# Stick-breaking scores: keys held once as high and low part, queries as two operands of 128 rows

## The chip, the cores and the metric

The kernel runs on one core of a Trainium2 chip. The metric is the time of one execution on the device in microseconds (us). Five engines work from queues of their own: TensorE (PE; its weight loads are listed as PEld), VectorE (DVE), ScalarE (ACT), GpSimd (POOL) and SyncE (SP), which issues most of the DMAs.

## The reference

One hybrid decoder block on x of (1, 1024, 1024): an RMS norm, one input projection, eight heads of strictly causal stick-breaking attention beside eight heads of latent attention (MLA), an output projection, a gated MLP with a short convolution, and a gated embedding. The part that the change touches is the score z of the stick-breaking heads:

```python
def stick_breaking_attention(q, k, v):
    scale = SB_HEAD_DIM ** -0.5                       # SB_HEAD_DIM = 64
    for start in range(0, seq, Q_BLOCK):              # 8 blocks of 128 queries
        end = start + Q_BLOCK
        z = jnp.einsum('bqhd,bkhd->bhqk', q[:, start:end], k[:, :end]) * scale
        strict = s_idx < t_idx
        log_keep = jnp.where(strict, -jax.nn.softplus(z), 0.0)
        log_keep_after = lax.cumsum(log_keep, axis=3, reverse=True) - log_keep
        weights = jnp.where(strict, jnp.exp(jax.nn.log_sigmoid(z) + log_keep_after), 0.0)
        outs.append(jnp.einsum('bhqk,bkhd->bqhd', weights, v[:, :end]))
```

## The kernel before

Every float32 operand of a product is held as the sum of two float32r parts, high and low (`split`, L90: ACT casts the high part at L93, DVE subtracts it from the source at L94). A product of two such operands is high by high, low by high and high by low. `mm3` (L115) does it in three matmuls.

Stage 1 (L203) normalises and transposes x into `hTh` and `hTl`, makes the latents, and the keys and values of the first pair of heads. Stage 2 begins with the stick-breaking heads: four pairs c of heads, each with two heads e, each with two halves g of the queries, which makes 16 units in the order c, e, g. `sb_softmax` (L624) makes the weights of a unit, one block of 128 queries after the other: the scores go to a PSUM bank (L636, L637 and, for the piece with the diagonal, the mask of L447), ACT takes two sigmoids of them (L640, L641), DVE scans the first along the keys (L643) and multiplies (L645). `weighted_sum` (L451) transposes the weights (L459), splits them (`th`, `tl`) and multiplies them with the values (L473, L474); DVE writes the unit's output `o` (L479), and after the last unit of a pair POOL sends it to the DRAM (L674). `run_units` writes the scores of a unit between the steps of the weighted sum of the unit before it.

Into the steps of both, `fill` mixes other work by rates: `project` (L224), which makes 128 columns of the input projection in 24 matmuls for each half `th` of the tokens, for the queries, keys and values of the next pair (`to_q`, `to_k`, `to_v`; `sb_pre`, L651, adds the three), and `mla_prepare` (L546). The last order on each engine is set by a scheduler from priorities; a fill has its priority put off by `LATER`.

The head dimension is 64, so a pair's projection holds head 0 in partitions 0 to 63 and head 1 in 64 to 127 (`hs`). For head e before the change, the key tile `ka` or `kb` has the high part of the keys in both halves of its 128 partitions (the second is a copy, L259), the low parts of both heads lie in a third tile `kl`, which takes its slot from the tag `ka` or `kb` by turns, and the query tile `qa` or `qb` has the high part in the head's own half and the low part in the other. The first product (L636) takes all 128 rows, which is high by high and low by high; the second (L637) takes the 64 rows of the head, high by low:

```python
pe.matmul(sc, q[:, qs], k[:, c0:c1], start=True, stop=False)               # L636
pe.matmul(sc, q[rows, qs], kl[rows, c0:c1], start=False, stop=c1 < n)      # L637
```

The MLA heads follow (stage 2, second part), with scores of 96 rows in three products (L1064 to L1066) and the same mask line L447; then the MLP and the embedding. The change doesn't touch these.

Of the kernel before, what the change touches and what calls it, by code (L numbers as in the profile page):

```python
# [18 lines left out]
P = 128  # L19
S = 1024  # L20
D = 1024
NT = 8          # token tiles
NK = 8          # chunks of D_MODEL
H = 512         # tokens of a half
HD = 64
DFF = 2816
NCH = DFF // P  # 22
# [8 lines left out]
# how the work between the steps of the attention is spread: steps of it per step  # L36
# [5 lines left out]
# how far the scheduler is to put it behind the attention  # L42
LATER = (500, 0, 0, 2000)
# tiles normalised together in each half, and those scaled on the scalar engine
# [5 lines left out]
def tile_hybrid_block(ctx: ExitStack, tc: tile.TileContext, a: dict, out: bass.AP):  # L50
# [39 lines left out]
    def split(h, l, src, gain=None, on_pool=False):  # L90
        """src (times a gain of each partition) as the sum of two float32r parts."""
        if gain is None:
            act.copy(h, src)  # L93
            (pool if on_pool else dve).tensor_tensor(l, src, h, ALU.subtract)  # L94
        else:
            act.activation(h, src, AF.Copy, scale=gain)
            dve.scalar_tensor_tensor(l, src, gain, h, ALU.mult, ALU.subtract)
# [9 lines left out]
    def split_w(src, width=512, gain=None, on_pool=False, where=None):  # L107
        """A weight block of the DRAM, split."""
        w = load_w(src, width)
        wh = (where or stage).tile([P, 512], F32R, tag="wh", name=nm("wh"), bufs=4)  # L110
        wl = (where or stage).tile([P, 512], F32R, tag="wl", name=nm("wl"), bufs=4)
        split(wh[:, :width], wl[:, :width], w[:, :width], gain, on_pool)
        return wh, wl
# [6 lines left out]
    def rstd_dve(small, ssq, count, n, tag, bufs=None):  # L120
        """(ssq / count + eps) ** -0.5 on one engine: Newton steps from a guess by exponent."""
# [16 lines left out]
    def rotate(eng, p_, x1, x2, cs, sn, shape):  # L138
        """The rotation of the pairs (x1, x2), in place."""
# [11 lines left out]
    class Fill:  # L151
        """Work traced in small steps between those of a stage. A generator gives True where it
        leaves none of the stage's buffers open."""
# [6 lines left out]
        def add(self, g, later=0):  # L160
            """later: how far behind the rest the scheduler is to put this work."""
            self.gens.append((g, later))
# [32 lines left out]
    now = {}                    # the current stage's makers of banks and of small tiles  # L195
# [17 lines left out]
    def sb_tiles(c):  # L213
        """Keys of two heads twice, their low parts, values; queries come later."""
        t4 = lambda tag: ata.tile([P, S], F32R, tag=tag, name=nm(tag), bufs=3)
        ka, kb = t4("ka"), t4("kb")
        kl = t4("ka" if c % 2 == 0 else "kb")
        vt = [ata.tile([P, NT, P], F32R, tag="v", name=nm("v"), bufs=3) for _ in range(2)]
        return {"k": (ka, kb), "kl": kl, "v": vt}
# [4 lines left out]
    def project(ci, consume, ths=(0, 1), ws=None):  # L224
        """128 columns of the input projection, transposed, for each half of the tokens."""
# [16 lines left out]
    def to_q(tiles):  # L242
        """Queries: the high part beside the low part."""
        def consume(th, ps):
            if th == 0:
                tiles["q"] = (tile4("qa", 2), tile4("qb", 2))
            sl = slice(th * H, th * H + H)
            for e in range(2):
                q = tiles["q"][e]
                split(q[hs[e], sl], q[hs[1 - e], sl], ps[hs[e], :])  # L250
        return consume

    def to_k(tiles):
        def consume(th, ps):
            sl = slice(th * H, th * H + H)
            for e in range(2):
                k = tiles["k"][e]
                split(k[hs[e], sl], tiles["kl"][hs[e], sl], ps[hs[e], :])
                act.copy(k[hs[1 - e], sl], k[hs[e], sl])  # L259
# [17 lines left out]
    with tc.tile_pool(name="pre", bufs=1) as pre, \  # L277
# [29 lines left out]
        # masks (rows are queries, columns keys)  # L307
# [7 lines left out]
        def normed(th):  # L315
            """A half of the tokens normalised, transposed and split."""
# [28 lines left out]
        # rotary tables  # L345
# [38 lines left out]
        def latents(th):  # L384
            """The latents of a half of the tokens, normalised, their keys' part rotated."""
# [14 lines left out]
            # the narrower part's sum doubled, so that one mean serves both  # L400
# [48 lines left out]
    def weighted_sum(u, p_, ptr, pav, rate):  # L449
        """The transposed product of a unit's weights with its values."""  # L450
# [30 lines left out]
        # the columns divided by their sums of weights: a row of each, the same in every partition  # L481
# [8 lines left out]
    def run_units(units, softmax, p_, ptr, pav, rates):  # L490
        """Softmax of each unit traced between the steps of the sum before it."""
# [52 lines left out]
    def mla_prepare(kv_only):  # L544
        """Latents to keys, values (kv_only) or queries of all MLA heads, kept in the DRAM."""
# [66 lines left out]

    for z in (project(0, to_q(pairs[0])), mla_prepare(False)):
# [10 lines left out]
    def sb_softmax(u):  # L624
        rows = hs[u["e"]]
        g, w = u["g"], u["w"]
        z = u["tiles"]
        q, k, kl = z["q"][u["e"]], z["k"][u["e"]], z["kl"]
        for i in range(4 * g, 4 * g + 4):
            n = (i + 1) * P  # L630
            qs = slice(i * P, i * P + P)
            kc = kcs[flip[0] % 2]
            flip[0] += 1
            for c0, c1 in pieces(n):
                sc = one_bank(py, "sc")[:, :c1 - c0]
                pe.matmul(sc, q[:, qs], k[:, c0:c1], start=True, stop=False)  # L636
                pe.matmul(sc, q[rows, qs], kl[rows, c0:c1], start=False, stop=c1 < n)  # L637
# [13 lines left out]
    def sb_pre(u):  # L651
        c, g, e = u["c"], u["g"], u["e"]
        if e == 0 and g == 0:
            fill.drain()
            sb_pre.o = atb.tile([P, S], F32, tag="o", name=nm("o"), bufs=2)
            if c < 3:
                z = sb_tiles(c + 1)
                pairs.append(z)
                for ci, f_ in ((c + 1, to_q), (c + 5, to_k), (c + 9, to_v)):
# [25 lines left out]
    # --- MLA heads; between them the output projection of the stick-breaking heads, then of the  # L685
    # --- MLA heads' first half of the tokens, then the FFN of this half
# [11 lines left out]
    def group_ssq(src, sq, s, ps):  # L698
        """Sums of the squares over the features of (128, 4, 128) in token layout."""
# [6 lines left out]
    def o_tile(c0, t):  # L706
        """Four chunks of features of a token tile."""
# [4 lines left out]
    def group_rstd(c0, ts):  # L712
        """Reciprocal roots of the mean squares of a group of features, one column a tile."""
# [13 lines left out]
    def group_product(c0, ts, consume):  # L727
        """A group of features times its rows of w_o."""
# [22 lines left out]
    def out_proj_sb(th, rows):  # L751
        """The stick-breaking heads' part of the output projection for a half of the tokens."""
# [8 lines left out]
    def out_proj_mla(th, rows, h2):  # L761
        """The rest of the output projection for a half of the tokens, residual and norm."""
# [40 lines left out]
    def embed(th, z):  # L803
        """Per-layer embeddings of a half of the tokens, kept in the DRAM."""
# [34 lines left out]
    def by_turns(a_, b_, rate):  # L839
        """Two generators, rate steps of the second for one of the first."""  # L840
# [9 lines left out]
    def f_tile(c):  # L850
        """A slot for a chunk of the FFN's hidden features (in pairs where a slot holds two)."""
# [13 lines left out]
    def ffn_up(th, h2, f):  # L865
# [10 lines left out]
        for c in range(NCH):  # L876
# [46 lines left out]
            if now.get("light"):  # L923
                # the same function with the tables that are loaded
# [12 lines left out]
    with tc.tile_pool(name="mla", bufs=1, side="right", reuse_waits="tile") as ml:  # L937
# [3 lines left out]
        # what the first unit needs lies where the stick-breaking heads are done early  # L941
# [4 lines left out]
        def mt(tag, shape, dt, bufs):  # L946
            """A tile of one of the bufs slots tag0, tag1 ... by turns; the first with the
            early ones."""
# [193 lines left out]
    def norm_transposed(row, t, dst):  # L1142
        """A normalised token tile, transposed and split."""
# [11 lines left out]
    def residual(row, xt, gain, dst):  # L1155
        """x + norm(row) * gain, kept in row and stored."""
# [67 lines left out]
    # the gate's weights stay on chip: some blocks in the stage, the rest where the FFN was  # L1224
# [117 lines left out]
```

## Time and profile before

| | us |
|---|---|
| median of 3 runs (1587.54 to 1591.46) | 1590.11 |
| span of the profiled execution, first to last instruction; the page gives no other time of it | 1588.5 |
| PE busy in the span | 1507.7 (95%) |
| DVE busy in the span | 1079.6 (68%) |
| ACT busy in the span | 844.2 (53%) |
| stick-breaking units, first score product to last output | 104.4 to 418.3 |

Times in rows are counted from the start of the span. PE's matmuls are pipelined and their ends are modelled, so how long a matmul holds PE is better read from the start of one to the start of the next than from its own time. DVE and ACT work through their instructions one by one, so their busy times are work.

### The profile page before, as it was taken

What the parts mean: (1) busy time and instruction counts of PE and PEld (TensorE: products, weight loads), DVE (VectorE), ACT (ScalarE), POOL (GpSimd) and SP (SyncE); (2) the same over time, 40 slices, a digit from 0 to 9 for tenths busy, and PEclk for the clock granted to TensorE, in tenths of its full rate; (3) what the DMA queues carried; (4) which work ended last, traced back from release to release, by engine and by line L of the source; (5) the groups of instructions that cost most, each with busy time, mean ns of one, the idle gap of its engine ahead of it and who ended that gap; (6) DMA issues with size and microseconds to landing.
All of it is one profiled execution on the core that took longest, in us unless ns stands there. A gap on an engine that the chain in (4) does not pass through costs nothing. (4 is left out here: it accounts for less than half of the span.)

```text
span 1588.5 us, 20809 instructions
## 1 busy us (share of the span) xinstructions
PE 1507.7 (95%) x7032; PEld 1214.6 (76%) x7032; DVE 1079.6 (68%) x2021; ACT 844.2 (53%) x1649; POOL 271.1 (17%) x313
## 2 busy tenths in 40 slices
PE   4998999999899897999999999999999999999996
PEld 3976877766678786778888888888888888888875
DVE  4558667799767868866567954544986556544698
ACT  6345555677667756645544544444554444444542
POOL 7104300002133425242113100000000000000033
PEclk9998999999889999999999999999999999999998
DMA  6031210113345525134445532333443323333455
GB/s 197 22 100 40 86 48 27 41 52 126 111 134 148 157 70 186 61 99 146 148 125 169 177 119 90 97 95 96 141 134 94 98 94 94 93 93 94 132 176 169
DMA packets 109211, 173.78 MB, mean 109 GB/s; under 512 B 10912, under 2 KB 47680, under 8 KB 109104
## 3 DMA queue, kind: packets, MB, share of 16 engines
q1 hardware_dynamic: 100400, 142.71, 29.7%
q0 software_dynamic: 8704, 29.74, 5.0%
q8 instruction: 55, 0.90, 0.2%
q14 instruction: 52, 0.43, 0.1%
HBM read 142.26 MB, written 30.15 MB: 109 GB/s over the span
## 5 line engine op out<-in xcount | busy, mean ns | idle before, releaser
L93 ACT CAST wh<-ws 128x512 fp32r<-128x512 f32 x296 | 183.1, 620 | 213.3 <-PE mm L891 105.8
L94 DVE TENSOR_TENSOR wl<-ws,wh 128x512 fp32r<-128x512 f32 x281 | 199.9, 713 | 139.7 <-ACT wh L93 74.5
L889 PE MATMUL mm<-bh,wh 128*128 128x512 f32 x456 | 180.2, 395 | 0.0
L891 PE MATMUL mm<-bh,wh 128*128 128x512 f32 x456 | 180.1, 395 | 0.0
L94 DVE TENSOR_TENSOR fl<-f,fh 128x512 fp32r<-128x512 f32 x88 | 60.7, 691 | 118.0 <-PE mm L118 77.4
L94 DVE TENSOR_TENSOR tl<-tr,th 128x512 fp32r<-128x512 f32 x192 | 103.2, 549 | 33.9 <-ACT th L93 32.8
L895 PE MATMUL mm<-bh,wl 128*128 128x512 f32 x456 | 126.0, 396 | 0.0
L93 ACT CAST th<-tr 128x512 fp32r<-128x512 f32 x192 | 90.7, 483 | 64.6 <-PE tr L459 49.4
L643 DVE TENSOR_TENSOR_SCAN kc<-kc,one_f 128x128 f32<-128x128 f32 (+3 forms) x64 | 89.2, 1394 | 36.4 <-ACT kc L640 35.7
L93 ACT CAST fh<-f 128x512 fp32r<-128x512 f32 x88 | 54.6, 622 | 110.0 <-PE mm L117 84.3
L1160 POOL DMA_DIRECT2D x_dram<-fd x8 | 4.3, 538 | 615.1 <-DVE fd L1159 582.2
L459 PE MATMUL tr<-ident,w 128*128 128x128 f32 x576 | 103.3, 290 | 4.4 <-DVE tl L94 2.0
L889 PEld LDWEIGHTS mm<-bh,wh 128*128 128x128 f32 x456 | 85.9, 188 | 19.9
L891 PEld LDWEIGHTS mm<-bh,wh 128*128 128x128 f32 x456 | 85.9, 188 | 19.9
L895 PEld LDWEIGHTS mm<-bh,wl 128*128 128x128 f32 x456 | 85.6, 188 | 19.7
L116 PE MATMUL mm<-wh,fh 128*128 128x512 f32 x242 | 95.6, 396 | 0.0
L117 PE MATMUL mm<-wl,fh 128*128 128x512 f32 x242 | 95.3, 394 | 0.0
L459 PEld LDWEIGHTS tr<-ident,w 128*128 128x128 f32 x576 | 74.8, 148 | 20.0 <-DVE tl L94 3.7
L474 PE MATMUL av<-tl,v 128*128 128x512 f32 x192 | 75.8, 398 | 13.8 <-DVE tl L94 13.1
L473 PE MATMUL av<-th,v 128*128 128x512 f32 x192 | 79.2, 412 | 6.6 <-ACT th L93 3.6
L118 PE MATMUL mm<-wh,fl 128*128 128x512 f32 x242 | 82.5, 395 | 0.0
L640 ACT ACTIVATE kc<-sc 128x384 f32<-128x384 f32 (+4 forms) x96 | 47.7, 496 | 38.3 <-PE sc L447 22.9
(427 smaller groups left out, 3833.2 us busy)
## 6 DMA issues: line engine op xcount, KB each, us to landing
ws<-in_w_up SPq DMA_DIRECT2D x176, 256.0 KB, 2.6
ws<-in_w_down SPq DMA_DIRECT2D x88, 256.0 KB, 2.6
ws<-in_w_o SPq DMA_DIRECT2D x32, 256.0 KB, 2.8
xl<-x_dram SPq DMA_DIRECT2D x16, 512.0 KB, 3.9
ws<-in_w_in SPq DMA_DIRECT2D x24, 256.0 KB, 2.7
t<-o_dram SPq DMA_DIRECT2D x24, 256.0 KB, 3.2
xl<-o_dram SPq DMA_DIRECT2D x24, 256.0 KB, 2.8
xt<-in_x SPq DMA_DIRECT2D x8, 512.0 KB, 5.3
```

The lines of the kernel that those rows point to most:

```text
L93: act.copy(h, src)
L94: (pool if on_pool else dve).tensor_tensor(l, src, h, ALU.subtract)
L116: pe.matmul(ps, lh, rh, start=start, stop=False)
L117: pe.matmul(ps, lh, rl, start=False, stop=False)
L118: pe.matmul(ps, ll, rh, start=False, stop=stop)
L459: pe.transpose(tr[:, c:c + P], w[i][:, j * P:(j + 1) * P], ident)
L473: pe.matmul(av[:, lo:], v(j), th[:, lo:], start=j == 0, stop=False)
L474: pe.matmul(av[:, lo:], v(j), tl[:, lo:], start=False, stop=j == last)
L643: dve.tensor_tensor_scan(rev, rev, one_f[:, 0:1].to_broadcast([P, n]), 1.0, ALU.mult, ALU.mult)
L889: pe.matmul(ps, wh[:, k * P:(k + 1) * P], nh[:, kk], start=kk == 0, stop=False)
L891: pe.matmul(ps, wh[:, k * P:(k + 1) * P], nl[:, kk], start=False, stop=False)
L895: pe.matmul(ps, wl[:, k * P:(k + 1) * P], nh[:, kk], start=False, stop=kk == NK - 1)
```

## The change

Keys are held once: the key tile of a head has the high part in the head's own half of the partitions and the low part in the other half; the third key tile and the copies of L259 are gone. Queries are held in two tiles: `qz` has the high part in the head's own half and zeros in the other, and `q` has the low part in the head's own half and the high part in the other, for which `to_q` has a new copy by ACT out of PSUM. The first product, `qz` by keys, is high by high; the second, `q` by keys, is low by high plus high by low. Both take 128 rows. The three parts of the product are as before.

The six `qz` tiles (three for each head of a pair, each for a half of the queries) are zeroed once by POOL and used in turn. In the fill the projection of the queries of the next pair now comes last. Two small things go with it: the output tile `o` has one buffer, not two, and each of the tags `ka`, `kb` has two, not three. The rest of the differences are comments.

```diff
     def sb_tiles(c):
-        t4 = lambda tag: ata.tile([P, S], F32R, tag=tag, name=nm(tag), bufs=3)
-        ka, kb = t4("ka"), t4("kb")
-        kl = t4("ka" if c % 2 == 0 else "kb")
+        ks = [ata.tile([P, S], F32R, tag=tag, name=nm(tag), bufs=2) for tag in ("ka", "kb")]
         vt = [ata.tile([P, NT, P], F32R, tag="v", name=nm("v"), bufs=3) for _ in range(2)]
-        return {"k": (ka, kb), "kl": kl, "v": vt}
+        return {"c": c, "k": ks, "v": vt}
...
             if th == 0:
                 tiles["q"] = (tile4("qa", 2), tile4("qb", 2))
+                tiles["qz"] = [[high_q[e][(2 * tiles["c"] + g) % 3] for g in range(2)]
+                               for e in range(2)]
             sl = slice(th * H, th * H + H)
             for e in range(2):
-                q = tiles["q"][e]
-                split(q[hs[e], sl], q[hs[1 - e], sl], ps[hs[e], :])
+                q, z = tiles["q"][e], tiles["qz"][e][th]
+                split(z[hs[e], :], q[hs[e], sl], ps[hs[e], :])
+                act.copy(q[hs[1 - e], sl], ps[hs[e], :])
...
                 k = tiles["k"][e]
-                split(k[hs[e], sl], tiles["kl"][hs[e], sl], ps[hs[e], :])
-                act.copy(k[hs[1 - e], sl], k[hs[e], sl])
+                split(k[hs[e], sl], k[hs[1 - e], sl], ps[hs[e], :])
...
+    high_q = [[atb.tile([P, H], F32R, name=f"qz{e}{i}") for i in range(3)] for e in range(2)]
+    for e in range(2):
+        for z in high_q[e]:
+            pool.memset(z[hs[1 - e], :].bitcast(F32), 0.0)
...
-        q, k, kl = z["q"][u["e"]], z["k"][u["e"]], z["kl"]
+        q, qz, k = z["q"][u["e"]], z["qz"][u["e"]][g], z["k"][u["e"]]
...
-                pe.matmul(sc, q[:, qs], k[:, c0:c1], start=True, stop=False)
-                pe.matmul(sc, q[rows, qs], kl[rows, c0:c1], start=False, stop=c1 < n)
+                pe.matmul(sc, qz[:, zs], k[:, c0:c1], start=True, stop=False)
+                pe.matmul(sc, q[:, qs], k[:, c0:c1], start=False, stop=c1 < n)
...
-            sb_pre.o = atb.tile([P, S], F32, tag="o", name=nm("o"), bufs=2)
+            sb_pre.o = atb.tile([P, S], F32, tag="o", name=nm("o"), bufs=1)
...
-                for ci, f_ in ((c + 1, to_q), (c + 5, to_k), (c + 9, to_v)):
+                for ci, f_ in ((c + 5, to_k), (c + 9, to_v), (c + 1, to_q)):
```

The order of the instructions moves on PE, ACT, DVE, POOL and SP within the stick-breaking units and the first MLA units; behind these it is the same. The number of instructions is the same on every engine but POOL, which has the six memsets more. In the changed file the lines stand a few numbers off: L642 and L643 are the score products (before L636, L637), L449 the mask (L447), L646 and L647 the sigmoids (L640, L641), L253 the new copy, L267 the copy of the values (L265).

On PE at the start of the first pair's first unit (`sc` a bank of scores, `ka` a key tile, `qa` and `qz` query tiles), before:

```order
L636 MATMUL sc_1270<-ka_99,qa_949 128x128
L637 MATMUL sc_1270<-ka_101,qa_949 128x128
L447 MATMUL sc_1270<-mask_sb,ident_r 128x128
L636 MATMUL sc_1278<-ka_99,qa_949 128x256
L541 MATMUL pj_1021<-ident,lt_1019 128x128 x4
L637 MATMUL sc_1278<-ka_101,qa_949 128x256
```

and now:

```order
L642 MATMUL sc_1280<-ka_99,qz_907 128x128
L643 MATMUL sc_1280<-ka_99,qa_956 128x128
L449 MATMUL sc_1280<-mask_sb,ident_r 128x128
L642 MATMUL sc_1288<-ka_99,qz_907 128x256
L643 MATMUL sc_1288<-ka_99,qa_956 128x256
L449 MATMUL sc_1288<-mask_sb,ident_r 128x128
```

Both products now read the same key tile, `ka_99`; the count of matmuls stays, and the place is the same.

On PE where the second pair's first scores stand (`pj` with `hTh`, `hTl` is a projection of that pair: 1595 the keys of the second half of the tokens, 1707 values), before:

```order
L459 MATMUL tr_2005<-ident,w_293_1671 128x128
L117 MATMUL pj_1595<-hTl_98,wh_1510 128x512
L118 MATMUL pj_1595<-hTh_96,wl_1511 128x512
L636 MATMUL sc_1924<-ka_1261,qa_1366 128x128
L637 MATMUL sc_1924<-kb_1263,qa_1366 128x128
L447 MATMUL sc_1924<-mask_sb,ident_r 128x128
L636 MATMUL sc_1971<-ka_1261,qa_1366 128x256
L637 MATMUL sc_1971<-kb_1263,qa_1366 128x256
L447 MATMUL sc_1971<-mask_sb,ident_r 128x128
L116 MATMUL pj_1595<-hTh_96,wh_1510 128x512
```

and now (1813 is the queries of the second half, the last of the six groups of that pair):

```order
L117 MATMUL pj_1813<-hTl_98,wh_1721 128x512
L118 MATMUL pj_1813<-hTh_96,wl_1722 128x512
L116 MATMUL pj_1813<-hTh_96,wh_1721 128x512
L117 MATMUL pj_1813<-hTl_98,wh_1721 128x512
L642 MATMUL sc_1933<-ka_1272,qz_909 128x128
L642 MATMUL sc_1978<-ka_1272,qz_909 128x256
L118 MATMUL pj_1813<-hTh_96,wl_1722 128x512
L116 MATMUL pj_1813<-hTh_96,wh_1721 128x512
L117 MATMUL pj_1813<-hTl_98,wh_1721 128x512
L118 MATMUL pj_1813<-hTh_96,wl_1722 128x512
L643 MATMUL sc_1933<-ka_1272,qa_1790 128x128
L449 MATMUL sc_1933<-mask_sb,ident_r 128x128
```

The first score of the second pair stood behind the queries and three quarters of the keys, and now stands behind keys, values and queries: 62 instructions further down PE's queue (instruction 853, before 791). For the third pair it is 56 (1197, before 1141), for the fourth 16 (1503, before 1487).

On ACT in the same place (`qa`, `qb`, `qz` are written by `to_q`; `th` are weights, `wh` a weight block, `v` values), before:

```order
L93 CAST qa_1366<-pj_1387 64x512
L93 CAST qb_1367<-pj_1387 64x512
L93 CAST th_1949<-tr_1942 128x512
L93 CAST th_1986<-tr_1953 128x384
L93 CAST ka_1261<-pj_1514 64x512
L259 COPY ka_1261<-ka_1261 64x512
L93 CAST kb_1262<-pj_1514 64x512
L259 COPY kb_1262<-kb_1262 64x512
```

and now:

```order
L93 CAST qz_907<-pj_1813 64x512
L646 ACTIVATE kc_1267<-sc_1933 128x128
L647 ACTIVATE w_331_1865<-sc_1933 128x128
L646 ACTIVATE kc_1269<-sc_1978 128x256
L647 ACTIVATE w_332_1866<-sc_1978 128x256
L253 CAST qa_1790<-pj_1813 64x512
L93 CAST qz_910<-pj_1813 64x512
L253 CAST qb_1791<-pj_1813 64x512
L646 ACTIVATE kc_1267<-sc_2016 128x384
```

The copies have moved from the keys to the queries. A new copy (L253) writes the tile that DVE's subtraction (L94) writes too, and waits for it; the sigmoids of the pair's next scores stand behind it in ACT's queue.

## Rows read from the trace of the kernel before

**Rows 1.** Windows: busy us (instructions) of each engine, granted clock, DMA share, GB/s.

```profile
core 0: us, PE busy (x) PEld busy (x) DVE busy (x) ACT busy (x) POOL busy (x), PEclk, DMA share, GB/s
100.00:160.00 60.00, 54.84 (x240) 42.04 (x238) 45.45 (x51) 35.45 (x81) 20.34 (x35) 0.86 0.17 47
160.00:340.00 180.00, 179.68 (x846) 136.06 (x845) 130.35 (x179) 108.62 (x231) 15.76 (x24) 1.00 0.16 50
340.00:420.00 80.00, 71.16 (x327) 49.80 (x328) 70.32 (x95) 53.22 (x118) 13.29 (x22) 0.91 0.25 85
```

**Rows 2.** Windows of line L637 alone, PE and PEld, the same stretches.

```profile
100.00:160.00 60.00, 10.53 (x22) 4.43 (x22) 0.86 0.17 47
160.00:340.00 180.00, 21.23 (x49) 8.94 (x49) 1.00 0.16 50
340.00:420.00 80.00, 11.88 (x26) 4.79 (x26) 0.91 0.25 85
```

**Rows 3.** Timeline of PE, one stick-breaking block: start us, us, engine line operation.

```profile
199.08 0.34 PE L636 MATMUL sc<-ka,qa 128*128 128x384 f32 x1
199.35 0.44 PE L637 MATMUL sc<-kb,qa 64*128 64x384 f32 x1
199.72 0.33 PE L447 MATMUL sc<-mask_sb,ident_r 128*128 128x128 f32 x1
199.89 0.45 PE L636 MATMUL sc<-ka,qa 128*128 128x512 f32 x1
```

**Rows 4.** Timeline of PEld, the load of that block's second product.

```profile
199.35 0.18 PEld L637 LDWEIGHTS sc<-kb,qa 64*128 64x128 f32 x1 [0.31 <-issue]
```

**Rows 5.** Timeline of PE, one MLA block of the same 384 columns.

```profile
511.15 0.33 PE L1064 MATMUL sc<-kt,qh 96*128 96x384 f32 x1
511.32 0.34 PE L1065 MATMUL sc<-kt,qh 96*128 96x384 f32 x1
511.49 0.34 PE L1066 MATMUL sc<-kt,ql 96*128 96x384 f32 x1
511.67 0.23 PE L447 MATMUL sc<-mask_ml,ident_r 128*128 128x128 f32 x1
511.73 0.45 PE L116 MATMUL pj<-wh,pe 128*128 128x512 f32 x1
```

**Rows 6.** Timeline of PEld, the load of that MLA block's second product.

```profile
511.15 0.19 PEld L1065 LDWEIGHTS sc<-kt,qh 96*128 96x128 f32 x1
```

**Rows 7.** Waits of DVE, 100 to 160: us in total, times, longest.

```profile
DVE kc L643 <- ACT kc L640: 8.2, 7, 2.0
```

**Rows 8.** Waits of DVE, 160 to 340.

```profile
DVE kc L643 <- ACT kc L640: 27.6, 15, 4.7
```

**Rows 9.** Waits of DVE, 340 to 420.

```profile
DVE kc L643 <- ACT kc L640: 1.0, 3, 0.6
```

**Rows 10.** Windows of all engines, the end of the middle stretch.

```profile
320.00:340.00 20.00, 20.00 (x102) 14.40 (x100) 16.85 (x26) 14.62 (x31) 0.00 (x0) 1.00 0.16 47
```

**Rows 11.** Waits of ACT, 100 to 420.

```profile
ACT qb L93 <- DVE qa L94: 8.4, 7, 1.7
```

**Rows 12.** Lines of ACT, 100 to 420, by form: count, busy us, mean ns, idle before.

```profile
L93 ACT CAST qa<-pj 64x512 fp32r<-64x512 f32 x7 | 4.1, 580 | 0.0
L259 ACT CAST ka<-ka 64x512 fp32r<-64x512 f32 x6 | 3.7, 618 | 0.2
```

**Rows 13.** Lines of POOL by form: the nearest memset.

```profile
L310 POOL MEMSET mf<- 128x128 f32 x2 | 0.4, 224 | 0.0
```

**Rows 14.** Timeline of POOL, its idle time ahead of the first rotation.

```profile
131.47 1.50 POOL L141 TENSOR_TENSOR rt<-qt,sin_t 128x128 f32<-128x128 f32 x1 [43.09 <-ACT qt L604]
```

**Rows 15.** Timeline of DVE: last output of the third pair, first of the fourth.

```profile
375.64 0.68 DVE L479 TENSOR_TENSOR o<-av,tmp 64x512 f32<-64x512 f32 x1
...
385.24 0.66 DVE L479 TENSOR_TENSOR o<-av,tmp 64x512 f32<-64x512 f32 x1
```

**Rows 16.** The tile o: landing of its DMAs.

```profile
DMA to landing us min/median/max: 2.3/2.8/6.4
```

More of the change, by code (lines that the diff above doesn't have):

```diff
@@ L624, in sb_softmax @@
     def sb_softmax(u):
-        rows = hs[u["e"]]
         g, w = u["g"], u["w"]
         z = u["tiles"]
-        q, k, kl = z["q"][u["e"]], z["k"][u["e"]], z["kl"]
+        q, qz, k = z["q"][u["e"]], z["qz"][u["e"]][g], z["k"][u["e"]]
         for i in range(4 * g, 4 * g + 4):
@@ L631, in sb_softmax @@
             qs = slice(i * P, i * P + P)
+            zs = slice((i - 4 * g) * P, (i - 4 * g) * P + P)
             kc = kcs[flip[0] % 2]
```

## Prediction, made before the changed kernel ran

> **What bounds the kernel now.** Start with the windows of the stick-breaking units, the only part whose work changes [rows 1]. See three stretches. From 160 to 340 us PE is busy 179.68 of 180 us while DVE has work for 130.35 (72%): PE is the bound. From 340 to 420 DVE is busy 70.32 of 80 us (88%) and PE gets 327 instructions done against 846 in the 180 us before: the last pairs have little fill and hang on DVE's scans. From 100 to 160 it is mixed: PE 54.84 and DVE 45.45 of 60, with the clock granted at a mean of 0.86, so part of it ran at 1.2 and not 2.4 GHz. The waits of DVE say the same: the scan waited for ACT's sigmoid, which had waited for scores, 8.2 us in the first stretch, 27.6 us in the second and 1.0 us in the last [rows 7 to 9].
>
> Next, what a score block costs PE. The timeline of a block of 384 keys shows starts at 199.08 (first product, 128 rows), 199.35 (second, 64 rows), 199.72 (mask), and the next block at 199.89: 0.81 us in all [rows 3]. The weights of the 64-row product are loaded at 199.35, the moment at which its matmul starts, after 0.31 us in which the loader stood with no releaser to be seen [rows 4]. Compare an MLA block of the same 384 columns, 96 rows in every product: starts at 511.15, 511.32, 511.49, the mask at 511.67, the next at 511.73 [rows 5]. There a product takes 0.17 us and the mask 0.06, and the second product's weights are loaded at 511.15, under the first product [rows 6]. So the 64-row product costs its neighbours and itself the overlap.
>
> **The change, part by part.**
>
> *The second product takes 128 rows.* In the MLA form two products and a mask would take 2 x 0.17 + 0.06 = 0.40 us instead of 0.81: 0.41 us less. For 512 columns it is about the same, since the excess is a standstill and not columns; a block without a mask saves less, and at the slow clock more. I take 0.40 for each. The trace counts the 64-row products by stretch: 22, 49 and 26 [rows 2] (one too many, at an edge). That is 8.8, 19.6 and 10.4 us of PE's time, 38.8 together. No row here shows two 128-row products of one bank whose key tile is the same; its bounds are 0 (the standstill stays) and 0.40, and I take 0.40, by the nearest row [rows 5], where three products of one bank with 96 rows have no gap.
>
> What of this is on the path? Middle: all, as long as DVE keeps up. If the 180 us shrink by 19.6, DVE's 130.35 become 81%. But from 320 to 340 DVE is already at 16.85 of 20 [rows 10]; of the eight or so products there I count half, so 45 x 0.40 = 18. First stretch: DVE stands 8.2 us for scores [rows 7], about as much as PE saves, but part of the stretch hangs on DVE; I take 6 of 8.8 (bounds 0 and 8.8). Last stretch: DVE waits for scores 1.0 us in all [rows 9]; I take 2 of 10.4 (bounds 0 and 10.4).
>
> *ACT's copies.* 16 copies of a key part (618 ns, from SBUF) go, 16 of a query part (about 580 ns by the cast out of PSUM) come [rows 12]: nothing. But the new copy waits for DVE's subtraction into the same tile. Before, each half of queries or keys had one such wait for DVE, between its two heads; now a half of queries has two, eight more in all. The row beside it: 8.4 us in 7 waits, 1.2 each [rows 11], so 9.6 us of ACT's time. Behind it in ACT's queue stand sigmoids, for which DVE's scan waits. ACT is busy 60% in the middle [rows 1], so most is covered; if the cover is gone it is all 9.6. I take 3 us (bounds 0 and 9.6).
>
> *Queries last in the fill.* The first scores of pairs two to four stand 62, 56 and 16 instructions further down PE. The fill that they now wait for is not new, it has only changed places with them, so while PE is the bound it costs nothing: what DVE lacks at the start of a pair it finds later, with less fill between the scores. It is a rival below.
>
> *The memsets.* A memset of 128 columns takes 224 ns [rows 13]; six of 512 columns are 6 x 0.9 = 5.4 us by columns, less if most is fixed cost. POOL stands idle 43.09 us before 131.47, that is from 88.4 [rows 14], and the units begin after 100: covered (uncovered, up to 5.4).
>
> *One output buffer.* The first output of a pair now waits until the last pair's tile has left. Closest are the third and fourth pair: last write 375.64, next 385.24, 9.6 us apart [rows 15], against a landing of 2.8 us, 6.4 at most [rows 16]. Covered; if POOL's queue delays it, some 3 us once, and it would be DVE that stands.
>
> *Fewer key buffers and reused `qz`.* Of two key tiles for each tag, one is read while the next is filled. A `qz` tile is overwritten by a projection that stands behind its last reader on PE. Nothing.
>
> Sum: 18 + 6 + 2 - 3 = 23 us. Behind the units the order is the same and PE leads (95% of the span in the table), so it goes through to the end: 1588.5 - 23 = 1565.5 for the profiled execution. Its span lies 1.6 us under the median of the runs, 1590.1; in terms of the runs that is 1567.
>
> **The rivals.**
>
> *No gain: a load still waits.* The loader stands before L637, and nothing in the row names the releaser. If it stands because a load cannot pass a matmul that uses the same rows, two 128-row products share all rows, and it stands on. Then PE saves nothing, ACT's waits cost 3, and the time is 1593. Against it: in the MLA block loads of 96 rows pass matmuls of 96 rows [rows 5, 6]. The Trainium skill ("TensorE: Matmul & The Clock Gate", Part 3, The mechanism) has it that a weight load overlaps with matmuls in flight only when the row group differs. By that rule the gain is zero; the trace disagrees, with a load at 511.15 under a matmul of 511.15 to 511.48 in the same rows. Chance 0.06.
>
> *Slower: DVE starves at the start of each pair.* Place: PE's queue ahead of the first scores of pairs two to four, which now stand behind the queries. Price: 62 + 56 + 16 = 134 instructions at 180 us / 846 = 0.21 us each [rows 1] is 28 us in which DVE gets no scans. If DVE sets the end of the units over all, half of the middle's gain and the last stretch's 2 go too: 28 + 3 for ACT - 9 - 6 = +16, or 1606. It decides once DVE's share in the middle, 72% now, rises to nearly all of the time between the starts of pairs. For it: the last 80 us already hang on DVE. Against: 50 us of DVE's 180 are idle now, and PE has them all. Chance 0.06.
>
> *DVE takes over early.* The saved PE time is half lost in the middle (9), the first stretch gives 3 and the last nothing: 12 us, 1578. Chance 0.13.
>
> *All of it.* PE's 38.8 us come through, and the first stretch loses some of its slow clock (0.86 of 60 us is 8 us under full speed; I take 3): 1548. Chance 0.05.
>
> **How the numbers follow.** My forecast, 1567, has 0.70. Its own ends: 12 us in the middle with 2 at the ends and 5 for ACT is 9 (1581); 19.6 with 8.8, 9 and none for ACT is 37 (1553). The range 1553 to 1581 takes in the third rival and leaves out the first two and the last, 0.17. A measurement of this kernel can tell some 0.3% (4.8 us) from no change: faster 0.70 + 0.13 + 0.05 = 0.88, same 0.06, slower 0.06.
>
> **What would show it.** In the changed profile the loads of the second score product start with the first product's matmul and the loader's waits ahead of it are gone; from start to start a block of 384 columns with its mask takes 0.40 us. The middle stretch, to the same place in PE's order, is some 18 us shorter with DVE above 78%, and the last stretch is as long as before within 3 us. ACT's waits for DVE at the new copy add up to about 10 us. The prediction is wrong if the load still stands, if DVE idles for more than 10 us ahead of a pair's first scores without PE being short of time elsewhere, or if the stretches before 100 or after the first MLA units change by more than 3 us.

## The result, and the profile after

The changed kernel takes 1578.76 us (median of 4 runs, 1576.29 to 1584.88) against 1589.34 beside it (4 runs): a ratio of 0.9938, 95% interval 0.9914 to 0.9962, so 10.6 us less. The forecast was 23 us less. The time lies in the range and near the third rival's number, but not for that rival's reason. The profiled execution is the longest of the four (span 1583.1 us), so positions inside the stick-breaking units are compared from the first scan on, not from the span's end. Of all runs in this document one, of late_all_no_gap below, fell in a slow state (2067.91 us at a mean granted clock of 0.654) and is left out of its numbers.

The windows of the changed kernel, the stretches of [rows 1]:

```profile
core 0: us, PE busy (x) PEld busy (x) DVE busy (x) ACT busy (x) POOL busy (x), PEclk, DMA share, GB/s
100.00:160.00 60.00, 51.01 (x273) 43.78 (x271) 50.88 (x60) 42.04 (x93) 27.42 (x37) 0.95 0.18 52
160.00:340.00 180.00, 166.99 (x837) 137.29 (x836) 128.79 (x176) 103.94 (x228) 11.88 (x23) 0.97 0.14 45
340.00:420.00 80.00, 67.67 (x360) 53.45 (x359) 68.95 (x104) 58.51 (x134) 18.29 (x25) 0.91 0.37 124
```

Look at the middle line. PE, which had no free moment there before, is now idle 13 us, and DVE is not busier for it: 128.79 us against 130.35. Neither engine is full. Time saved on PE turned into waiting.

Next, did the wider product do its part? The timeline of PE, a block of 384 columns with its mask, and the next product behind it, as in [rows 3]:

```profile
221.96 0.33 PE L642 MATMUL sc<-ka,qz 128*128 128x384 f32 x1
222.12 0.34 PE L643 MATMUL sc<-ka,qa 128*128 128x384 f32 x1
222.31 0.22 PE L449 MATMUL sc<-mask_sb,ident_r 128*128 128x128 f32 x1
222.37 0.45 PE L118 MATMUL pj<-hTh,wl 128*128 128x512 f32 x1
```

From start to start it is 0.16, 0.19 and 0.06, in all 0.41 us in place of 0.81. The timeline of the loader shows the second product's weights at 221.96, with the first product's matmul and with no wait ahead [rows 4, 6]:

```profile
221.96 0.19 PEld L643 LDWEIGHTS sc<-ka,qa 128*128 128x128 f32 x1
```

So the standstill is gone as forecast. What took its gain back stands in DVE's timeline: the last scan of the first pair (1024 columns), and the first scans of the second.

```profile
153.62 2.56 DVE L649 TENSOR_TENSOR_SCAN kc<-kc,one_f 128x1024 f32<-128x1024 f32 x1 [0.32 <-ACT kc L646]
...
205.39 0.99 DVE L649 TENSOR_TENSOR_SCAN kc<-kc,one_f 128x128 f32<-128x128 f32 x2
```

That pause of 51.8 us between starts was 30.9 us before:

```profile
163.78 2.37 DVE L643 TENSOR_TENSOR_SCAN kc<-kc,one_f 128x1024 f32<-128x1024 f32 x1
194.63 0.42 DVE L643 TENSOR_TENSOR_SCAN kc<-kc,one_f 128x128 f32<-128x128 f32 x1 [0.76 <-ACT kc L640]
```

Between the second and third pair it grew from 2.5 to 19.8, between the third and fourth from 4.6 to 13.2. While DVE pauses, PE runs the fill (from 153 to 205 us it is busy 49.14 of 52); when the scans come, that fill is used up, and PE waits. PE's waits in the changed kernel, 160 to 340 us (total us, times, longest), where it had waited 0.3 us in all before (`tr` is a bank of transposed weights, `tl` their low part, `av` the bank in which a unit's weighted sum is made):

```profile
PE av L476 <- DVE tl L94: 5.1, 7, 1.3
PE tr L461 <- DVE tl L94: 3.8, 2, 2.1
PE av L475 <- DVE o L481: 2.3, 1, 2.3
```

What the loss consists of can be read for the second pair, from the first pair's last output to its own. The change (first line) and form_alone, a kernel of the next section with the wide product and the old order (second line), give PE about as many matmuls in it:

```profile
191.80:302.33 110.53, 103.55 (x517) 85.36 (x516) 77.39 (x106) 65.97 (x145) 0.55 (x1) 0.97 0.10 32
195.66:297.14 101.48, 100.90 (x520) 84.84 (x519) 79.48 (x107) 66.36 (x144) 0.55 (x1) 1.00 0.11 37
```

The stretch is 9.1 us longer: PE is idle 7.0 us in place of 0.6, and the granted clock has a mean of 0.97 in place of 1.00, which is 3.4 us of full speed. The two stand together in time. PE waits 4.5 us in all between 259.7 and 265.4, and from 263.3 to 270.1 its granted clock is 0.50, the lower of its two levels (1.2 GHz). Between 240 and 270 us PE has 39 projection matmuls of the fill to do in the change, and 85 in form_alone.

DVE's own wait for the sigmoids fell, as PE's faster scores should make it, from 27.6 to 10.6 us in that stretch [rows 8]. ACT's wait at the new copy, 100 to 420 us, is small [rows 11]:

```profile
ACT qa L253 <- DVE qa L94: 2.7, 5, 0.9
ACT qb L253 <- DVE qb L94: 1.1, 2, 0.8
```

### The profile page after: what moved, and what is told of

It reads as the page before. It is cut to its first block, busy times and chain, and to the rows that moved or that the text cites. A ratio compares the mean times of both kernels' runs of the same rounds, so it can differ in the third digit from the quotient of the medians.

```text
span 1583.1 us, 20827 instructions
## 1 busy us (share of the span) xinstructions
PE 1479.8 (93%) x7032; PEld 1212.8 (77%) x7032; DVE 1075.7 (68%) x2021; ACT 841.2 (53%) x1649; POOL 279.1 (18%) x319
## 5 line engine op out<-in xcount | busy, mean ns | idle before, releaser
L94 DVE TENSOR_TENSOR wl<-ws,wh 128x512 fp32r<-128x512 f32 x281 | 203.9, 727 | 147.4 <-ACT wh L93 84.2
L94 DVE TENSOR_TENSOR fl<-f,fh 128x512 fp32r<-128x512 f32 x88 | 60.8, 692 | 117.9 <-PE mm L118 77.4
L94 DVE TENSOR_TENSOR tl<-tr,th 128x512 fp32r<-128x512 f32 x192 | 103.2, 550 | 45.3 <-ACT th L93 41.8
L897 PEld LDWEIGHTS mm<-bh,wh 128*128 128x128 f32 x456 | 85.9, 188 | 19.8
L901 PEld LDWEIGHTS mm<-bh,wl 128*128 128x128 f32 x456 | 85.6, 188 | 19.8
L649 DVE TENSOR_TENSOR_SCAN kc<-kc,one_f 128x128 f32<-128x128 f32 (+3 forms) x64 | 88.0, 1381 | 13.1 <-ACT kc L646 12.9
L116 PE MATMUL pj<-hTh,wh 128*128 128x512 f32 x160 | 65.6, 410 | 0.0
```

Source lines behind the costliest of these rows:

```text
L116: pe.matmul(ps, lh, rh, start=start, stop=False)
L649: dve.tensor_tensor_scan(rev, rev, one_f[:, 0:1].to_broadcast([P, n]), 1.0, ALU.mult, ALU.mult)
L897: pe.matmul(ps, wh[:, k * P:(k + 1) * P], nl[:, kk], start=False, stop=False)
L901: pe.matmul(ps, wl[:, k * P:(k + 1) * P], nh[:, kk], start=False, stop=kk == NK - 1)
```

## The experiments

**Theory "order".** The wide product gives PE its time, and the queries' place at the end of the fill takes part of it back, since a pair's scans then start later. **Rivals.** DVE bounds the units whatever the order; ACT's new waits take it; the three shared tiles `qz` make the queries wait. To compare profiles I use two numbers from DVE's timeline and the tile `o`: the pauses between one pair's last and the next pair's first scan, and the length of the units, from the start of the first scan to the start of the last output (before: 107.4 to 417.6, 310.2 us). The whole set, ratios against the kernel before, timed beside each:

| kernel | ratio, 95% interval | pauses, us | units, us |
|---|---|---|---|
| before | 1 | 30.9, 2.5, 4.6 | 310.2 |
| the change | 0.9938, 0.9914 to 0.9962 | 51.8, 19.8, 13.2 | 298.6 |
| form_alone | 0.9887, 0.9863 to 0.9911 | 35.8, 4.2, 4.6 | 287.6 |
| order_alone | 1.0021, 1.0001 to 1.0041 | 45.7, 15.6, 12.7 | 315.2 |
| queries_second | 0.9887, 0.9863 to 0.9910 | 38.6, 2.5, 5.1 | 289.1 |
| copy_first | 0.9966, 0.9947 to 0.9985 | 49.4, 15.5, 16.6 | 299.7 |
| late_pair2_only | 0.9933, 0.9913 to 0.9954 | 51.8, 2.2, 2.5 | 298.6 |
| slots_alone | 0.9940, 0.9920 to 0.9961 | 53.2, 19.6, 11.8 | 298.3 |
| late_pairs3and4 | 0.9858, 0.9837 to 0.9879 | 37.2, 14.7, 11.9 | 291.3 |
| weights_on_pool | 0.9903, 0.9882 to 0.9924 | 39.2, 2.4, 5.2 | 291.3 |
| query_products_late | 0.9866, 0.9843 to 0.9889 | 2.2, 2.2, 2.6 | 283.2 |
| late_all_no_gap | 0.9906, 0.9878 to 0.9934 | 19.5, 2.2, 13.1 | 290.8 |

**form_alone** and **order_alone** split the change in two. The first:

```diff
-pe.matmul(sc, q[rows, qs], kl[rows, c0:c1], start=False, stop=c1 < n)
+pe.matmul(sc, q[:, qs], kl[:, c0:c1], start=False, stop=c1 < n)
```

> The kernel before with one edit: the second score product reads all 128 rows of the query tile and of the low-part tile (so it adds the other head's rows, and the scores are other numbers; the work per instruction is that of the change). Fill order, copies and buffers stay as before. Theory 'order' (the wider product gives PE some 30 us, and the queries' place at the end of the fill takes two thirds of it back, because the first scan of each pair comes later): the gain is much larger than the change's 10.6 us, 18 to 28 us, 1561 to 1571, and the pause of DVE's scans between the first and the second pair stays at about 31 us or less. Rival 'DVE bounds the units' (PE's time is off the path whatever the order): 8 to 12 us, 1577 to 1581, as the change itself. Rival 'ACT's new waits eat it' (3.8 us in all at the new copy): 3 to 5 us better than the change, 1574 to 1576.

It took 1568.29 us, 1.13% or 17.9 us less than before (14.1 to 21.7 by the interval): at the lower end of "order", and outside both rivals. The pause is 35.8 us, not the 31 or less expected, since the first pair's scans end earlier. Its windows in the middle show both engines doing more than in the change, PE 175.43 and DVE 140.93 of 180 us:

```profile
160.00:340.00 180.00, 175.43 (x902) 146.44 (x902) 140.93 (x197) 116.22 (x254) 15.84 (x28) 0.98 0.17 56
```

The second, the kernel before with `(c + 5, to_k), (c + 9, to_v), (c + 1, to_q)` as the fill's order:

> The kernel before with one edit: the fill of a pair projects keys, values, queries instead of queries, keys, values; the 64-row product stays. Theory 'order': DVE's pause between the first and the second pair grows from 31 to 50 us or more, and the kernel gets slower than before by 8 to 20 us, 1597 to 1609. Rival 'DVE bounds the units' and rival 'ACT's new waits': the order costs nothing while PE is the bound, 1586 to 1592.

It took 1591.05 us, 0.21% more (0.01 to 0.41): 3.3 us. The pauses grew by 36 us in all (the first to 45.7, short of the 50 expected), nearly the 40 from form_alone to the change, but the price is far under the 8 to 20 expected. With the narrow product PE is so full that a late scan costs little: in the units it idles 14.5 us, against 12.8 before. With the wide one it idles 30.5 us in the change against 24.7 in form_alone, and the same order costs 0.9938 against 0.9887, some 8 us. Each price alone is uncertain by 3 to 5 us, so the difference rests on the whole table: the wide kernels with late queries in the second pair are at 0.9933 to 0.9966 (the change, slots_alone, late_pair2_only, copy_first), those without at 0.9858 to 0.9903 (form_alone, queries_second, late_pairs3and4, weights_on_pool), on the mean 9.5 us apart. The two parts of the change don't add up: the first makes the second dear. The first pause of order_alone:

```profile
163.07 2.38 DVE L643 TENSOR_TENSOR_SCAN kc<-kc,one_f 128x1024 f32<-128x1024 f32 x1
208.78 1.01 DVE L643 TENSOR_TENSOR_SCAN kc<-kc,one_f 128x128 f32<-128x128 f32 x2
```

**queries_second** keeps the change and moves the queries ahead of the values; **slots_alone** has its tiles alone:

```diff
-for ci, f_ in ((c + 5, to_k), (c + 9, to_v), (c + 1, to_q)):
+for ci, f_ in ((c + 5, to_k), (c + 1, to_q), (c + 9, to_v)):
...
-tiles["qz"] = [[high_q[e][(2 * tiles["c"] + g) % 3] for g in range(2)]
+tiles["qz"] = [[high_q[e][(2 * tiles["c"] + g) % len(high_q[e])] for g in range(2)]
...
-high_q = [[atb.tile([P, H], F32R, name=f"qz{e}{i}") for i in range(3)] for e in range(2)]
+high_q = [[atb.tile([P, H], F32R, name=f"qz{e}{i}") for i in range(2 + 2 * e)] for e in range(2)]
```

> The changed kernel with the fill in the order keys, queries, values; so that the queries may come earlier, the head whose scores come last has four tiles qz and the other two (six as in the change). Nothing is left out. Theory 'order': the first scan of the second pair comes at 180 to 190 us instead of 205.4, and the kernel takes 1560 to 1570. Rival 'DVE bounds the units': 1576 to 1581, as the change. Rival 'ACT's new waits': also 1576 to 1581, since the copies wait as before.

> The changed kernel with the queries still last, but with two and four tiles qz for the two heads in place of three and three, as in queries_second. Nothing is left out. Theory 'order': the tiles don't matter, 1575 to 1582, as the change. Rival 'the shared tiles qz make the queries wait for the last scores that read them': 1566 to 1572, as queries_second.

queries_second took 1568.13 us, 17.9 less than before, all that form_alone had; the second pair's first scan comes at 189.74. slots_alone took 1578.75, a ratio of 0.9940 against the change's 0.9938. So the order it is, and not the tiles. And since queries_second keeps the new copies, the memsets and the fewer buffers, and still has form_alone's ratio, these cost nothing that the runs can tell. In queries_second DVE's pause is short again:

```profile
151.16 2.55 DVE L649 TENSOR_TENSOR_SCAN kc<-kc,one_f 128x1024 f32<-128x1024 f32 x1 [0.32 <-ACT kc L646]
189.74 0.42 DVE L649 TENSOR_TENSOR_SCAN kc<-kc,one_f 128x128 f32<-128x128 f32 x1 [1.38 <-ACT kc L646]
```

And PE has work through the whole second pair, as the window from its first scan to its last output shows:

```profile
190.00:293.00 103.00, 102.50 (x530) 86.30 (x529) 81.27 (x111) 66.77 (x146) 0.55 (x1) 1.00 0.11 37
```

530 matmuls, hardly any idle time. The same window of the change:

```profile
205.00:302.00 97.00, 90.02 (x454) 74.21 (x453) 72.77 (x99) 59.82 (x133) 0.00 (x0) 0.96 0.08 25
```

It has 76 matmuls less to do, since they ran before the scans, and is only 6 us shorter; PE is idle 7 us and its clock is granted at 0.96.

**copy_first** puts `act.copy(q[hs[1 - e], sl], ps[hs[e], :])` ahead of the `split` in `to_q`.

> The changed kernel with the new copy of the queries ahead of the split, so that ACT no longer waits for DVE's subtraction into the same tile (3.8 us in 7 waits there in the changed profile). Theory 'order' and rival 'DVE bounds the units': 0 to 2 us less than the change, 1576 to 1579. Rival 'ACT's new waits': 4 us or more less, 1575 or below.

It took 1582.27 us, 0.9966: no gain, a shade more than the change if anything. ACT's wait on DVE for this tile pair is 2.0 us in place of 3.8. ACT's waits were covered; that rival falls.

**late_pair2_only** and **late_pairs3and4** ask which pair pays. Edit, on top of queries_second: `(k_, v_, q_) if c == 0 else (k_, q_, v_)`, and `c > 0` for the other.

> As queries_second, but the second pair's queries alone are projected last, as in the change; those of the third and fourth pair come second. Nothing is left out. Theory 'order' (each pair whose queries come last starts its scans late and pays for it by itself): pair two costs most, since its scans then start some 15 us later (205 against 190), so about half of the 10.7 us between the change and queries_second: 1571 to 1576. Rival 'it is the tiles qz or the last pairs': 1568, as queries_second, if pairs three and four pay; 1579 if pair two pays for all.

> The complement of late_pair2_only: in the wide-product kernel the second pair's queries are projected second, those of the third and fourth pair last. Nothing is left out. Theory 'the loss is made where the longest fill stands ahead of late first scores, in pair two' (late_pair2_only lost nearly all): 1567 to 1572, near queries_second. Rival 'any late pair costs the whole, because the end of the units hangs on the last pairs': 1576 to 1580, as the change and as late_pair2_only.

The first took 1577.3 us (0.9933), nearly all of the loss, more than the half expected. The second took 1565.03 (0.9858), no loss at all. Late queries of the second pair cost the whole; those of the third and fourth are free. The traces show a difference between the places. Behind the first pair DVE has a pause of 37 us anyway, and some 15 us more are added to it (37.2 to 51.8). In late_pairs3and4 the third pair's scans start 9.0 us later after the kernel's first scan than in queries_second, and its last one only 0.7 us later: they are caught up inside the pair, since PE and DVE both have idle time there (from 293 to 358 us of queries_second PE is busy 57.60 of 65). That this is why they are free is argued from the traces, not shown by a run.

**before_light** and **after_light** cut DVE's product of weights and scans to 128 columns, some 33 us of its work (the columns behind are left out of the weighting):

```diff
-dve.tensor_tensor(w[i], w[i], kc[:, S - n + 1:S + 1], ALU.mult)
+dve.tensor_tensor(w[i][:, :P], w[i][:, :P], kc[:, S - n + 1:S - n + 1 + P], ALU.mult)
```

> The kernel before with DVE's product of weights and scans cut to the first 128 columns of each row tile: some 33 us of DVE's work in the stick-breaking units is left out, and the output with it. Theory 'order' with PE the bound before and DVE the bound behind the change: only the last 80 us, in which DVE was busy 88%, gain, 5 to 12 us, 1575 to 1582. Rival 'DVE bounds the units already before': 20 us or more.

> The changed kernel with the same cut of DVE's work, some 33 us. Theory 'order' (scans that start late, then DVE sets the pace to the end of the pair): the cut is worth much more than in the kernel before, 15 to 25 us, 1554 to 1564. Rival 'the loss is on PE, not on DVE': the cut is worth as much as in the kernel before, within 4 us.

They took 1576.69 us (0.9926, 0.9904 to 0.9949: 12.3 us less than before) and 1563.52 (0.9848, 0.9823 to 0.9873: 15.2 less than slots_alone, timed beside it). The totals don't tell the theories apart: 3 us between them is what the rival allowed. My expectation had left out the first pair, which hangs on DVE in both. By pairs there is a difference: from the first pair's last output to the third's, before_light is 181.2 us and before 176.0, so the cut gains nothing there; after_light is 166.2 and the change 173.2, so it gains 7. That fits "order", but a single profile of each is thin for it.

**weights_on_pool** gives POOL the 18 subtractions for the weights of the fill's projections (`split_w(..., on_pool=True)`), on top of queries_second.

> As queries_second, with DVE's 18 subtractions for the fill's projection weights (some 0.7 us each, 13 us) given to POOL, which took 1.37 us for the same form and stands idle most of the units. Nothing is left out. Theory 'DVE and the chain through it bound pair one and the last two pairs, PE the second': about half of the 13 us comes through, 1560 to 1566. Rival 'PE now waits for the weights' low parts, which come later': 1568 to 1574.

It took 1572.35 us (0.9903), within the interval of queries_second and not the gain expected. POOL took 1.36 us where DVE had taken 0.83, and DVE was rid of 15.0 us, of which 3.2 came back in longer scans and products. PE's list of waits has none on POOL, so the rival's reason is not seen either; why this brings nothing stays open. It fits a bound by the chain and not by DVE's load: 33 us cut from the products, which stand in the chain, gave 12 to 15 us, and 15 cut from work beside the chain gave none. That is argued from these runs, not shown. POOL's row here, and DVE's in queries_second (both lines of the window 100 to 420):

```profile
L94 POOL TENSOR_TENSOR wl<-ws,wh 128x512 fp32r<-128x512 f32 x18 | 24.4, 1359 | 83.2 <-ACT wh L93 71.5 <-PE sc L449 11.7
```

```profile
L94 DVE TENSOR_TENSOR wl<-ws,wh 128x512 fp32r<-128x512 f32 x18 | 15.0, 832 | 3.0 <-ACT wh L93 2.6 <-PE tr L461 0.2
```

**query_products_late** takes `mla_prepare(False)` out of the program ahead of the units and adds it to the fill behind `mla_prepare(True)`, the halves of the tokens one after the other. **late_all_no_gap** is the same with the queries last again.

> As queries_second, with the MLA queries' products (which stood ahead of and between the first units) moved into the fill of the fourth pair, where PE has some 18 of 80 us idle; the latents of the second half are read after the products of the first. Nothing is left out. Theory 'PE's idle time behind 320 us takes them': 6 to 14 us less than queries_second, 1554 to 1562. Rival 'their splits and copies meet a DVE that is busy there and delay the first MLA unit': 1568 to 1580.

> As query_products_late (whose scans have no pause between the first and the second pair: 170.7 to 172.9), but with the queries last in the fill of every pair, as in the change. Nothing is left out. Theory 'late queries cost only where DVE has run out of scans, which it does behind pair one alone, because the MLA queries' products crowd the fill out of that pair': they cost 0 to 4 us here, 1565 to 1572. Rival 'late queries of pair two always cost some 9 us': 1575 to 1579.

The first took 1567.44 us (0.9866): no worse than queries_second, none of the 6 to 14 us expected. The units are 5.9 us shorter (283.2), but the MLA queries now come right before the units that need them. Its pause behind the first pair is gone. The second took 1573.37 (0.9906), 0.40% or 6.4 us more than the first, with intervals that overlap. It lies between the two bands, so it settles for neither. Its premise failed: with the queries last the pause was back, since the first pair's scans ended earlier.

```profile
156.97 2.28 DVE L644 TENSOR_TENSOR_SCAN kc<-kc,one_f 128x1024 f32<-128x1024 f32 x1
176.44 0.42 DVE L644 TENSOR_TENSOR_SCAN kc<-kc,one_f 128x128 f32<-128x128 f32 x1
```

Read as a dose it agrees with the rest: 17 us more of pause cost 6.4 us here, 16 us more cost 8 between form_alone and the change. Both prices are uncertain by 5 to 6 us, so this is no more than agreement.

Three kernels beat both the one before and the change: queries_second, late_pairs3and4 and query_products_late, at 1565 to 1568 us. Their intervals overlap; which is best isn't settled.

## Why the prediction was wrong

**The step that failed** is "Queries last in the fill": "while PE is the bound it costs nothing: what DVE lacks at the start of a pair it finds later, with less fill between the scores". The sum put it at nothing; it costs some 8 us (0.9938 against form_alone's 0.9887). Of the 12.4 us between forecast and result this is one part; another 8 are the size of the wide product (26 us forecast, 17.9 measured), and the 3 put down for ACT were not spent. The condition is the weak place: the gain that the prediction counts on is just what ends PE's being the bound. With the narrow product, where PE is the bound, order_alone cost 3.3 us; with the wide one the same order cost more than twice that. The fill that runs ahead of the late scores is lost behind them, and PE waits there for DVE: for the low parts of the transposed weights, which end a chain from the scores over ACT's sigmoids, DVE's scan and product and PE's transposes, and once, 2.3 us, for an output that stood behind a scan in DVE's queue (264.66, behind the scan of 262.46). Behind the waits the clock falls, which is part of the price (3.4 us in the second pair).

**The wide product.** The mechanism was right: 0.41 us a block, the load with the first product's matmul. The size was somewhat high. The terms 6, 18 and 2 make 26 us; form_alone shortens the units by 22.6 us, the span of the profiled execution by 21.9 and the median of many runs by 17.9. By pairs (last output to last output) the 22.6 are 6.5, 10.8, 4.3 and 1.0: near the forecast at the ends, 6 and 2, and 15.1 instead of 18 between, though pairs and the forecast's stretches don't begin and end together. Two things made it smaller. A piece without a mask, a third of the 96, saves less: one of 384 columns takes on the mean 0.68 us before and 0.40 in form_alone, start to start at the full clock, against 0.86 and 0.43 with a mask. And of the time that PE gains in the units 12 us become idle time (12.8 us before, 24.7 in form_alone). The first rival, that a load still waits, falls: 0.16 us lie between the starts of two products of 128 rows with the same key tile. What stood there before came with the change between 64 and 128 rows, and widening alone took it away. The Trainium skill ("TensorEngine Tiling (Array Packing)", Tiling Modes, Key Properties) says that switching the tiling mode drains TensorE; the trace agrees, as far as it can tell a drain from another standstill: a masked block of 384 columns lost 0.40 us with its 64-row product (0.81 to 0.41). The prediction weighed another rule, on loads, and passed by this one.

**ACT's new waits**, 3 us of a bound of 9.6: 3.8 us in 7 waits, and nothing in the time (copy_first). **Memsets**: six at 521 ns, 2.9 us in all, covered; the first scan of the kernels with them comes at 104.8 to 109.6 us, 107.4 before. **One output buffer**: the fourth pair's first write comes 9.0 us after the third's last (364.3 and 373.3), and the DMA between them landed 3.0 us after its issue at 365.24; no wait, as forecast. **Key buffers and `qz`**: nothing (queries_second has the same key buffers, slots_alone other `qz`).

**The rivals.** The second had the place right, the queue ahead of the first scores. Its price was 28 us, and the scans did start late by more than that: the pauses are 40 us longer than in form_alone, over three pairs. But all three do not cost alike, the second pair pays for all. Its condition was wrong: it asked that DVE be nearly full, and DVE was at 72% in the middle. A pair that starts late runs, by PE's and DVE's waits, at the pace of a chain through three engines, and none of them has to be full. The third rival's number, 1578, was met for another reason than its own, that DVE takes over early.

Of what the prediction said would show it wrong, two lines came true. DVE idles for more than 10 us ahead of the second pair's first scores, 24 of the 49 us between the scans, and PE is not short of time elsewhere; but before the change it was already 12 of 31 us, so the line was badly drawn. And the stretch from the last MLA score to the end is 932.0 us in the changed kernel's profile against 925.5 before. Its order of work is the same, and it is 929.7 in slots_alone and 924.7 in form_alone, so this looks like the scatter between executions; no run settles it.

## What to carry to other kernels

A reordering is only free as long as the bound that hides it stands; where the same change removes that bound, cost the reordering against the profile that will be, not the one that is. Here it cost only in the second pair, where it lengthened a pause that was there already. Where two engines feed each other in a chain, the time at which the chain of a section starts counts, and work that fills the gap ahead of it is missing later; put what the chain's first step needs early in the fill, and what it needs last at its end. A product over fewer rows than its neighbours can cost more than the zeros that would make it whole: 64 rows among 128 did here, while the MLA products of 96 rows beside a mask of 128 show no such cost [rows 5].

## What was not expected of the hardware

POOL and DVE slow one another. In the changed kernel POOL's rotation of 128 columns took 2.46 us at 153.97, beside DVE's long scan (153.62, 2.56 us), and 0.45 right behind it:

```profile
153.97 2.46 POOL L142 TENSOR_TENSOR rt<-qt,sin_t 128x128 f32<-128x128 f32 x1
156.40 0.45 POOL L143 TENSOR_TENSOR qt<-qt,cos_t 128x128 f32<-128x128 f32 x1
156.82 0.45 POOL L144 TENSOR_TENSOR qt<-qt,cos_t 128x128 f32<-128x128 f32 x1
157.24 0.45 POOL L145 TENSOR_TENSOR qt<-qt,rt 128x128 f32<-128x128 f32 x1
157.65 0.45 POOL L146 TENSOR_TENSOR qt<-qt,rt 128x128 f32<-128x128 f32 x1
```

And DVE's product of 1024 columns took 2.62 us at 156.56, beside those rotations, against 1.21 at 394.04 with POOL idle:

```profile
156.56 2.62 DVE L651 TENSOR_TENSOR w<-w,kc 128x1024 f32<-128x1024 f32 x1
...
394.04 1.21 DVE L651 TENSOR_TENSOR w<-w,kc 128x1024 f32<-128x1024 f32 x1
```

The Trainium skill ("SBUF — State Buffer", Who interferes with whom) says that a VectorE instruction with two SBUF inputs contends with a GpSimd instruction that reads SBUF, since both need a shared pair of ports that is an exclusive lock. The trace agrees: the rotation that began at 153.97 ends at 156.43, right behind the scan's end at 156.18. The two don't take turns, though: DVE's product, which began at 156.56, ends at 159.18, about its own undisturbed 1.21 us behind the end of the last of four POOL instructions in a row (158.10). No run was made for it.
